# The first mixer of a two-layer kernel: short attention products to GpSimd, low parts of weights to VectorE, casts and two score levels to ScalarE, linear attention's outputs in four parts

## The chip, the cores and the metric

The kernel runs on one core of one Trainium2 chip. The metric is the device time of one execution in microseconds (us). The core has five engines that run their own queues in order and wait for each other by semaphores: TensorE (PE in the profile; its weight loads are PEld), VectorE (DVE), ScalarE (ACT), GpSimd (POOL) and SyncE (SP), which here issues nearly all DMA transfers.

## The reference, cut to what matters

The reference computes two transformer layers on 256 tokens of width 1024 (and 16 meta tokens ahead of them, so 272 rows). The first layer begins with a hybrid mixer, and only this mixer is touched by the change:

```python
proj = hn @ w_in                      # 1024 x 3088: sbq sbk sbv | gq gk gv gr glr
sb_o = stick_breaking_attention(...)  # 8 heads of 64
#   a = exp(log_sigmoid(z) + sum over later keys of log_sigmoid(-z)), strictly causal
lg = log_sigmoid(glr @ w_gate_up + b_gate_up) / 16
gla_o = gated_linear_attention(...)   # 4 heads, key width 64, value width 128
#   attn[t,s] = sum_d q[t,d] k[s,d] exp(bcum[t,d] - bcum[s,d]), causal;  o = attn @ v
gla_o = rmsnorm(gla_o, gla_norm_g) * silu(gr)
h = h + concat([rmsnorm(sb_o), gla_o]) @ w_out
```

After it come an expert layer (product keys, 16384 single-neuron experts, all of them multiplied through) and a second layer with window attention, a linear recurrence and a feed-forward part. All data is float32.

## The kernel before

**Weights as jobs.** Every weight matrix passes through as a stream of jobs of 128x1024 elements. A job is loaded by DMA into a buffer `raw` (four of them), split into a high part `whi` (a rounding cast to the type fp32r, line 194) and a low part `wlo = raw - whi` (a subtraction, line 196), and multiplied in three passes (lines 48 to 50: high by high, high by low, low by high). `whi` and `wlo` have three buffers each. A letter per job says who splits it: a lower-case letter puts the cast on ScalarE, an upper-case one on VectorE; `p` or `P` puts the subtraction on GpSimd, `v` or `V` on VectorE. In the first mixer the letters are the string in `lo_cycle(...)` of `plan_mixer1`, one per job; the mixer has 33 jobs: 4 for sbq, 4 for sbk, 4 for sbv, a small one for glr, 2 for gk, 2 for gq, 4 for gv, 4 for gr and 8 for `w_out` (called k=0 to k=7).

**Steps.** `st.step(mid)` runs one job. It first emits the copies that evacuate finished results, then loads up to the sixth job ahead and splits up to the second job ahead, and then emits the job's matmuls in two halves; between the halves it calls `mid`. So what stands in `mid`, and what stands behind the step, is woven between the matmul halves of TensorE's queue. The weaving is done with Python generators; `run(g)` emits one piece of g up to its next `yield`. The order of all queues is therefore fixed by the order of these calls.

**Attention** (`sb_units`, nine steps, jobs 8 to 16). There are 12 units, each one or two heads of one block of 128 queries. In each half step a unit passes a stage: scores on TensorE (line 458); sigmoid on ScalarE (431) and the causal mask on GpSimd (433, an affine select); one minus it, a running product over the keys on VectorE (440, 442) and the product with the shifted result (443); transposes on TensorE (450) and a small copy; and copies out of PSUM (422, 424, 425).

**Linear attention** (`gla`, eight steps, jobs 17 to 24). The 128x128 decay matrix of a block is built in levels: level v treats blocks of 2h columns, h = 2^v, and multiplies keys of the first half of each block with queries of the second half. A level has four stages in four successive half steps: differences `Dt` on VectorE (622) and two exponentials on ScalarE (623, 624); products `kq` with keys and queries (631, 632); 8 matmuls on TensorE into two PSUM banks (644); and two masked copies (`copy_predicated`, line 616) that put the level's entries into `AT`. The two PSUM banks of a level have only these two buffers, so the next level's matmuls wait for the copies. Between these pieces stands the output part of the first attention, `sb_out` (so), which multiplies weights with values (541, 546), and normalises (555 to 575), and `v_rows` (vr), which transposes gv (483).

**Outputs of linear attention** (`gla_out`). For each block of 128 rows and each of four heads it multiplies `Amt`, `AT` and for the second block `Axt` with values (694, 695, 697); then the rows are normalised in `head_norm` (470 to 475, the power on GpSimd at line 83), transposed (104) and split (112, 113) into `mixT`. The `w_out` job k=4 is the first that needs them; k=5 to 7 are held and multiplied at the end. Behind the mixer stand the residual addition (1078), the next norm, and the first jobs of the expert layer.

Of the kernel before, what the change touches and what calls it, by code (L numbers as in the profile page):

```python
# [14 lines left out]
ALU = mybir.AluOpType  # L15
# [149 lines left out]
class Job:  # L165
# [33 lines left out]
    def mm(self):  # L199
        self.f(self.W)  # L200
# [170 lines left out]
def lo_cycle(pat):  # L371
    while True:
        yield from pat
# [31 lines left out]
def sb_units(cx, sm, sbqT, sbkT, A0T, A1T, bm):  # L405
# [4 lines left out]
    nc = cx.nc  # L410
# [3 lines left out]
    for u in range(nu + 4):  # L414
# [11 lines left out]
        if 0 <= u - 1 < nu:  # L426
            i, hd = units[u - 1]
            n = 144 + 128 * i
# [6 lines left out]
        if 0 <= u - 2 < nu:  # L435
            i, hd = units[u - 2]
            n = 144 + 128 * i
            be = bs[u - 2]
            sc = sm.tile([128, 288], F32, tag="sc", name="sc", bufs=2)[:, :n * len(hd)].rearrange("p (h k) -> p h k", h=len(hd))
            nc.vector.tensor_scalar(out=sc, in0=be, scalar1=-1.0, scalar2=1.0, op0=ALU.mult, op1=ALU.add)  # L440
            for j in range(len(hd)):
                nc.vector.tensor_tensor_scan(sc[:, j, ::-1], sc[:, j, ::-1], cx.zero[:, :n], 1.0, ALU.mult, ALU.add)  # L442
            nc.vector.tensor_tensor(out=be[:, :, 0:n - 1], in0=be[:, :, 0:n - 1], in1=sc[:, :, 1:n], op=ALU.mult)
        if 0 <= u - 3 < nu:
            i, hd = units[u - 3]
            be = bs.pop(u - 3)
# [134 lines left out]
def gla(cx, sm, P, mk):  # L581
# [3 lines left out]
    nc = cx.nc  # L585
# [22 lines left out]
    def blocks(a, h):  # L608
        return a.rearrange("p a (n c) -> p (a n) c", c=2 * h)

    for lv in range(8 + 3):

        v = lv - 3
        if v >= 0:
            for b in range(2):
                nc.vector.copy_predicated(P.AT[:, b], mk[:, v, :].unsqueeze(1).broadcast_to((128, 4, 128)),
                                          pas.pop((v, b)).rearrange("p (a t) -> p a t", a=4))
        if lv < 7:
            h = 1 << lv
            Dt = sm.tile([128, 2, 256], F32, tag="Dt", name="Dt", bufs=2)  # L620
# [6 lines left out]
        if 0 <= v < 7:  # L627
            h = 1 << v
            kq = sm.tile([128, 2, 256], F32, tag="kq", name="kq", bufs=2)
            d, o = blocks(Ds.pop(v), h), blocks(kq, h)  # L630
            nc.vector.tensor_tensor(out=o[:, :, 0:h], in0=d[:, :, 0:h], in1=blocks(P.kR, h)[:, :, 0:h], op=ALU.mult)
            nc.vector.tensor_tensor(out=o[:, :, h:], in0=d[:, :, h:], in1=blocks(P.qR, h)[:, :, h:], op=ALU.mult)
            KQ[v] = kq, kq
        elif v == 7:
            KQ[v] = P.kR, P.qR
# [19 lines left out]
            nc.vector.tensor_tensor(out=km, in0=P.bm, in1=P.bm[:, :, 15:16].broadcast_to((128, 2, 16)), op=ALU.subtract)  # L655
            nc.scalar.activation(km, km, AF.Exp, scale=-S)
        if lv == 9:
            nc.vector.tensor_tensor(out=P.QE, in0=P.QE, in1=P.qR, op=ALU.mult)
            nc.vector.tensor_tensor(out=P.KE0, in0=P.KE0, in1=P.kR[:, :, 0:128], op=ALU.mult)
            km = P.KEm[:, :, 0, :]  # L660
            nc.vector.tensor_tensor(out=km, in0=km, in1=P.km, op=ALU.mult)
            nc.vector.tensor_tensor(out=P.KEm[:, :, 1, :], in0=km, in1=P.e0.unsqueeze(2).broadcast_to((128, 2, 16)), op=ALU.mult)
# [21 lines left out]
def gla_out(cx, sm, P, mixT):  # L684
    nc = cx.nc
    mm = nc.tensor.matmul
    pos = []
    for i in range(2):
        po = cx.bank("t")
        for h in range(4):  # L690
            vs = slice(128 * h, 128 * h + 128)
            o = po[:, vs]
            b, j = h % 2, h // 2
            mm(o, P.Amt[:, b, 2 * i + j, :], P.gvm[:, vs], start=(h == 0), stop=False, skip_group_check=True)
            mm(o, P.AT[:, b, 2 * i + j, :], P.gv[:, i, vs], start=False, stop=(h == 3 and i == 0), skip_group_check=True)
            if i == 1:
                mm(o, P.Axt[:, 2 * b + j, :], P.gv[:, 0, vs], start=False, stop=(h == 3), skip_group_check=True)
        pos.append(po)
    yield
    rw = [sm.tile([128, 512], F32, tag="rw", name="rw", bufs=4) for _ in range(2)]  # L700
    ns = [head_norm(cx, sm, pos[i], 4, 128, P.sg[:, i, :], rw[i]) for i in range(2)]
    for _ in range(2):
        for n in ns:
            run(n)
        yield
    for i in range(2):
        cx.dump(f"rowgl{i}", rw[i])
    pv = [cx.tr_pe(rw[i], 128) for i in range(2)]
    yield
    for i in range(2):  # L710
        cx.tr_split(pv[i], mixT, 4, 128 * i)


def plan_mixer1(cx, st, M):
    I = cx.I
    W = I["w_in"][0]
    nc = cx.nc
    lo = lo_cycle("pvpVpvpvPVVPVppVPPpvpPppPpPvppVVv")
    xT = lambda: M.hT
    tiles = lambda: [tuple(a[:, :, 16 + 128 * i:144 + 128 * i] for a in M.hT) for i in range(2)]  # L720

# [10 lines left out]
    def ev_g(i, ps):  # L732
        g, t = M.P.sg[:, i, :], cx.sm.tile([128, 512], F32, tag="rw", name="rw", bufs=4)
        nc.scalar.activation(g, ps, AF.Sigmoid)
        nc.vector.tensor_tensor(out=t, in0=ps, in1=M.ggl, op=ALU.mult)  # L735
        st.defer(lambda: nc.gpsimd.tensor_tensor(out=g, in0=g, in1=t, op=ALU.mult))


    def glr(W_):
# [20 lines left out]
def mixer1(cx, st, M, hx):  # L760

    nc, tc, I = cx.nc, cx.tc, cx.I
    if True:
# [93 lines left out]
        vr = v_rows(cx, M.vT, P.gv, P.gvm, "z")  # L857
        lc = lru_consts(cx)
        for n in range(8):
            st.step(adv(g, so) if n < 7 else adv(g))  # L860
            run(so if n < 6 else vr)
            run(g)
            run(lc)
        go = gla_out(cx, sm, P, M.mixT)
        st.step(adv(g))
        run(vr)
        run(g)
        for n in range(7):
            st.step(adv(go))
            run(go)  # L870
            if n == 3:
                g2 = peer_gain(cx)
        drain(go)
        peer_in(cx, st, M, hx, g2)
# [1000 lines left out]
```

## Time and profile before

| | us |
|---|---|
| Time before, median of 3 runs (lowest, highest) | 1306.52 (1304.94, 1306.63) |
| The profiled execution: its device time | 1307.48 |
| Its span, first to last instruction | 1305.8 |
| TensorE matmuls busy | 1246.6 (95%) |
| VectorE busy | 978.8 (75%) |
| ScalarE busy | 682.0 (52%) |
| GpSimd busy | 590.8 (45%) |

The device time holds 1.7 us that lie outside the span. All stretches below are in microseconds from the start of the span: the stick-breaking attention lies from about 36 to 84, the linear attention from 84 to 145, the `w_out` jobs with the linear attention's outputs from 145 to 181, and the expert layer begins at about 188.

### The profile page before, as it was taken

To read this page: it belongs to the slowest core of one execution; us is meant where nothing else is said; L and a number is where in the kernel's file an instruction comes from. 1 tells how busy PE (TensorE), PEld (TensorE's weight loads), DVE (VectorE), ACT (ScalarE), POOL (GpSimd) and SP (SyncE) were. 2 spreads that over 40 slices of the span, in tenths; PEclk is the share of its full clock that TensorE was granted. 3 is DMA by queue.
4 is the path that set the end of the run, shared out by engine and by line. 5 is a ranking of instruction groups with operands and counts; after the bars stand their busy time and mean duration, and the time that the engine had idled before them with its cause. 6 is when DMAs were issued, how large, how long until landed. Compare 5 with 4: busy or idle time off the path is not lost.

```text
span 1305.8 us, 23107 instructions
## 1 busy us (share of the span) xinstructions
PE 1246.6 (95%) x8724; PEld 1103.2 (84%) x8724; DVE 978.8 (75%) x1556; ACT 682.0 (52%) x1381; POOL 590.8 (45%) x291
## 2 busy tenths in 40 slices
PE   8988889989999999999999999999997989999998
PEld 7876679989999999998777788888886977999886
DVE  5778366998999888887899986555557887676444
ACT  5343244444456777776776774445544633545222
POOL 4433334778888777776666566000003342200101
PEclk9999799999999999999999999999998989899999
DMA  7431158656666656663554546765554423456653
GB/s 224 129 97 65 65 146 206 177 162 178 188 175 187 178 171 171 171 178 113 178 179 144 166 167 205 228 230 183 188 192 114 134 81 97 146 179 192 191 187 105
DMA packets 147292, 211.10 MB, mean 162 GB/s; under 512 B 17559, under 2 KB 121165, under 8 KB 147182
## 3 DMA queue, kind: packets, MB, share of 16 engines
q1 hardware_dynamic: 146844, 209.41, 53.3%
q8 instruction: 68, 1.11, 0.4%
q14 instruction: 42, 0.34, 0.1%
q10 hardware_dynamic: 338, 0.23, 0.1%
HBM read 207.35 MB, written 2.10 MB: 160 GB/s over the span
## 4 chain that ended last, share of the span: by engine, by line
PE 73%; DVE 11%; issue 7%; POOL 5%; ACT 2%; DMA 2%; SPq 0%; DVEq 0%; POOLq 0%; ACTq 0%
PE mm L48 22%; PE mm L49 22%; PE mm L50 22%; POOL wlo L196 3%; PE pg L1041 2%; POOL wlo L224 1%; DVE sc L442 1%; DVE whi L194 1%; DVE wlo L196 1%; PE z L1513 1%; DMA raw<-in_w_peer_q_dram 1%; DVE ut L215 1%; DMA g<-in_norm_g_dram 1%; PE t L644 1%; PE t L1531 1%
## 5 line engine op out<-in xcount | busy, mean ns | idle before, releaser
L196 POOL TENSOR_TENSOR wlo<-raw,whi 128x1024 fp32r<-128x1024 f32 x98 | 241.4, 2470 | 352.4 <-ACT whi L194 276.1
L224 POOL TENSOR_TENSOR wlo<-ut,whi 128x1024 fp32r<-128x1024 f32 x128 | 307.0, 2407 | 84.4 <-ACT whi L223 81.7
L194 ACT CAST whi<-raw 128x1024 fp32r<-128x1024 f32 x208 | 217.3, 1049 | 194.5 <-PE mm L50 154.4
L196 DVE TENSOR_TENSOR wlo<-raw,whi 128x1024 fp32r<-128x1024 f32 (+1 forms) x157 | 198.5, 1267 | 150.7 <-ACT whi L194 147.8
L50 PE MATMUL mm<-xTh,wlo 128*128 128x256 f32 x1088 | 305.1, 280 | 3.3 <-POOL wlo L224 3.3
L48 PE MATMUL mm<-xTh,whi 128*128 128x256 f32 x1088 | 306.5, 282 | 1.6 <-ACT whi L223 1.4
L49 PE MATMUL mm<-xTl,whi 128*128 128x256 f32 x1088 | 304.4, 280 | 0.3 <-DVE xTl L113 0.3
L49 PE MATMUL mm<-wlo,xTh 128*128 128x512 f32 x576 | 230.1, 400 | 4.2 <-POOL wlo L196 4.1
L48 PE MATMUL mm<-whi,xTh 128*128 128x512 f32 x576 | 232.1, 403 | 0.3 <-DVE rw L735 0.3
L50 PE MATMUL mm<-whi,xTl 128*128 128x512 f32 x576 | 229.1, 398 | 0.0
L50 PEld LDWEIGHTS mm<-xTh,wlo 128*128 128x128 f32 x1088 | 205.0, 188 | 3.9 <-POOL wlo L224 3.9
L48 PEld LDWEIGHTS mm<-xTh,whi 128*128 128x128 f32 x1088 | 204.6, 188 | 2.4 <-ACT whi L223 1.6
L49 PEld LDWEIGHTS mm<-xTl,whi 128*128 128x128 f32 x1088 | 205.0, 188 | 0.5 <-DVE xTl L113 0.5
L215 DVE STREAM_TRANSPOSE ut<-raw 128x1024 f32<-128x1024 f32 x128 | 158.7, 1240 | 39.2 <-POOL wlo L224 24.6
L223 ACT CAST whi<-ut 128x1024 fp32r<-128x1024 f32 x128 | 133.7, 1045 | 52.0 <-DVE ut L215 26.2
L1047 ACT ACTIVATE A<-A,w 128x64 f16<-128x64 f16 x512 | 129.1, 336 | 32.5 <-DVE A L1025 32.4
L49 PEld LDWEIGHTS mm<-wlo,xTh 128*128 128x128 f32 x576 | 109.4, 190 | 31.9 <-POOL wlo L196 7.2
L48 PEld LDWEIGHTS mm<-whi,xTh 128*128 128x128 f32 x576 | 109.4, 190 | 26.9 <-DVE rw L735 0.8
L50 PEld LDWEIGHTS mm<-whi,xTl 128*128 128x128 f32 x576 | 109.3, 190 | 26.6 <-DVE xTl L1210 0.4
L1210 DVE TENSOR_TENSOR xTl<-HS,xTh 128x256 fp32r<-128x256 f32 (+1 forms) x129 | 98.7, 767 | 3.3 <-ACT xTh L1206 3.3
L1114 ACT ACTIVATE HS<-mm 128x512 f32<-128x512 f32 x64 | 38.4, 599 | 86.5 <-PE mm L50 86.4
L1045 DVE TENSOR_TENSOR B<-kc,i 128x1024 f16<-128x1024 f32 x64 | 76.9, 1201 | 5.2 <-PE pg L1041 5.2
(394 smaller groups left out, 2059.5 us busy)
## 6 DMA issues: line engine op xcount, KB each, us to landing
raw<-in_expert_u_dram SPq DMA_DIRECT2D x512, 128.0 KB, 3.0
raw<-in_expert_v_dram SPq DMA_DIRECT2D x128, 512.0 KB, 3.5
raw<-in_w_ff_dram SPq DMA_DIRECT2D x64, 512.0 KB, 3.9
raw<-in_w_in_dram SPq DMA_DIRECT2D x38, 512.0 KB, 3.9
raw<-in_w_out_dram SPq DMA_DIRECT2D x16, 512.0 KB, 3.4
raw<-in_w_peer_q_dram SPq DMA_DIRECT2D x32, 128.0 KB, 4.4
h1d<-row SPq DMA_DIRECT2D x2, 512.0 KB
row<-h1d SPq DMA_DIRECT2D x2, 512.0 KB, 5.8
```

The lines of the kernel that those rows point to most:

```text
L48: mm(out, lhs[0], rhs[0], start=start, stop=False, skip_group_check=sk)
L49: mm(out, lhs[0], rhs[1], start=False, stop=False, skip_group_check=sk)
L50: mm(out, lhs[1], rhs[0], start=False, stop=stop, skip_group_check=sk)
L194: (nc.vector.tensor_copy if self.lo.isupper() else nc.scalar.copy)(hi[:, :n], self.raw[:, :n])
L196: eng.tensor_tensor(out=lo[:, :n], in0=self.raw[:, :n], in1=f32(hi[:, :n]), op=ALU.subtract)
L215: self.cx.nc.vector.transpose(self.ut, self.raw)
L223: nc.scalar.copy(ov(hi), pv(ut))
L224: nc.gpsimd.tensor_tensor(out=ov(lo), in0=pv(ut), in1=ov(f32(hi)), op=ALU.subtract)
L1045: nc.vector.tensor_tensor(out=B, in0=G.iota.unsqueeze(1).broadcast_to((128, 8, 128)), in1=bc(G.i2[:, c], 128), op=ALU.is_equal)
L1047: nc.scalar.activation(A[0][:, j, :], A[0][:, j, :], AF.Copy, scale=G.w1[:, t0 + j:t0 + j + 1])
L1114: st.defer(lambda: nc.scalar.activation(M.HS[b // NH][:, o - 1:o + 1, :].rearrange("p a t -> p (a t)"), ph, AF.Gelu))
L1210: nc.vector.tensor_tensor(out=wl[:, ts], in0=src(b, ts), in1=f32(wh[:, ts]), op=ALU.subtract)
```

## The change

Six edits, all in the first mixer:

- In `sb_units` the product of line 443 goes from VectorE to GpSimd (12 instructions of 271 or 286 elements per partition).
- In `gla` the two products `kq` of each of seven levels go from VectorE to GpSimd (14 instructions of 256 elements), and two later products, `QE` (512) and `KE0` (256).
- The masked copies of levels 5 and 6 become plain copies of the blocks that matter, on ScalarE: four of 32 partitions for level 5, two of 64 for level 6.
- The string of the weight splits changes from job 8 on: all casts on ScalarE; all subtractions on VectorE but for jobs 26, 28 and 29.
- The product of `sg` with its gain (line 736 before) goes from GpSimd to VectorE.
- `gla_out` yields after every second head, so its matmuls stand in four parts and not in one, and it begins one step earlier; `sb_out` and `v_rows` are woven in another order.

```diff
-            nc.vector.tensor_tensor(out=be[:, :, 0:n - 1], in0=be[:, :, 0:n - 1], in1=sc[:, :, 1:n], op=ALU.mult)
+            nc.gpsimd.tensor_tensor(out=be[:, :, 0:n - 1], in0=be[:, :, 0:n - 1], in1=sc[:, :, 1:n], op=ALU.mult)
...
-                nc.vector.copy_predicated(P.AT[:, b], mk[:, v, :].unsqueeze(1).broadcast_to((128, 4, 128)),
-                                          pas.pop((v, b)).rearrange("p (a t) -> p a t", a=4))
+                pa = pas.pop((v, b)).rearrange("p (a t) -> p a t", a=4)
+                if v in (5, 6):
+
+                    h = 1 << v
+                    for s in range(0, 128, 2 * h):
+                        nc.scalar.copy(P.AT[s:s + h, b, :, s + h:s + 2 * h], pa[s:s + h, :, s + h:s + 2 * h])
+                else:
+                    nc.vector.copy_predicated(P.AT[:, b], mk[:, v, :].unsqueeze(1).broadcast_to((128, 4, 128)), pa)
...
-            nc.vector.tensor_tensor(out=o[:, :, 0:h], in0=d[:, :, 0:h], in1=blocks(P.kR, h)[:, :, 0:h], op=ALU.mult)
-            nc.vector.tensor_tensor(out=o[:, :, h:], in0=d[:, :, h:], in1=blocks(P.qR, h)[:, :, h:], op=ALU.mult)
+            nc.gpsimd.tensor_tensor(out=o[:, :, 0:h], in0=d[:, :, 0:h], in1=blocks(P.kR, h)[:, :, 0:h], op=ALU.mult)
+            nc.gpsimd.tensor_tensor(out=o[:, :, h:], in0=d[:, :, h:], in1=blocks(P.qR, h)[:, :, h:], op=ALU.mult)
...
-            nc.vector.tensor_tensor(out=P.QE, in0=P.QE, in1=P.qR, op=ALU.mult)
-            nc.vector.tensor_tensor(out=P.KE0, in0=P.KE0, in1=P.kR[:, :, 0:128], op=ALU.mult)
+            nc.gpsimd.tensor_tensor(out=P.QE, in0=P.QE, in1=P.qR, op=ALU.mult)
+            nc.gpsimd.tensor_tensor(out=P.KE0, in0=P.KE0, in1=P.kR[:, :, 0:128], op=ALU.mult)
...
+            if h % 2:
+                yield
         pos.append(po)
-    yield
...
-    lo = lo_cycle("pvpVpvpvPVVPVppVPPpvpPppPpPvppVVv")
+    lo = lo_cycle("pvpVpvpv" + 17 * "v" + "vpvppvvv")
...
-        st.defer(lambda: nc.gpsimd.tensor_tensor(out=g, in0=g, in1=t, op=ALU.mult))
+        st.defer(lambda: nc.vector.tensor_tensor(out=g, in0=g, in1=t, op=ALU.mult))
...
-            st.step(adv(g, so) if n < 7 else adv(g))
-            run(so if n < 6 else vr)
+            st.step(adv(g, vr if n == 6 else so))
+            run(vr if n in (4, 5) else so)
             run(g)
             run(lc)
+        run(so)
+        drain(g)
         go = gla_out(cx, sm, P, M.mixT)
-        st.step(adv(g))
-        run(vr)
-        run(g)
-        for n in range(7):
+        for n in range(8):
             st.step(adv(go))
             run(go)
-            if n == 3:
+            if n == 4:
                 g2 = peer_gain(cx)
```

GpSimd's queue over the attention, before (`be` is a unit's weights, `wlo` a job's low part):

```order
L196 TENSOR_TENSOR wlo<-raw,whi 128x1024
L433 AFFINE_SELECT be<-be 128x128 x2
L196 TENSOR_TENSOR wlo<-raw,whi 128x1024
L433 AFFINE_SELECT be<-be 128x128 x3
L196 TENSOR_TENSOR wlo<-raw,whi 128x1024
L433 AFFINE_SELECT be<-be 128x128 x2
```

The same place in the changed kernel:

```order
L433 AFFINE_SELECT be<-be 128x128
L443 TENSOR_TENSOR be<-be,sc 128x271
L433 AFFINE_SELECT be<-be 128x128
L443 TENSOR_TENSOR be<-be,sc 128x271
L433 AFFINE_SELECT be<-be 128x128
L443 TENSOR_TENSOR be<-be,sc 128x271
```

The long subtractions are gone from this stretch, and a product of one unit now stands behind the mask of the next unit.

VectorE's queue in the step that takes the differences of levels 4 and 5, before:

```order
L622 TENSOR_TENSOR Dt<-bR 128x512
L631 TENSOR_TENSOR kq<-Dt,kR 128x32x8
L632 TENSOR_TENSOR kq<-Dt,qR 128x32x8
L616 COPY_PREDICATED AT<-mk,t 128x512 x2
L622 TENSOR_TENSOR Dt<-bR 128x512
L631 TENSOR_TENSOR kq<-Dt,kR 128x16x16
L632 TENSOR_TENSOR kq<-Dt,qR 128x16x16
```

The same place in the changed kernel (line 623 is the masked copy, 628 the difference, 1274 a constant of the second layer):

```order
L196 TENSOR_TENSOR wlo<-raw,whi 128x1024
L623 COPY_PREDICATED AT<-mk,t 128x512 x2
L628 TENSOR_TENSOR Dt<-bR 128x512
L623 COPY_PREDICATED AT<-mk,t 128x512 x2
L628 TENSOR_TENSOR Dt<-bR 128x512
L1274 SCALAR_TENSOR_TENSOR sp<-sp,z_1060 128x4 x2
L196 TENSOR_TENSOR wlo<-raw,whi 128x1024
```

The two products between two masked copies have left VectorE; once in two levels a subtraction of the weights stands ahead of a masked copy.

TensorE's queue at the outputs of linear attention, before (part of 20 short matmuls that stand in one run):

```order
L694 MATMUL t<-gvm,Amt 128x128
L695 MATMUL t<-gv,AT 128x128
L697 MATMUL t<-gv,Axt 128x128
L694 MATMUL t<-gvm,Amt 128x128
L695 MATMUL t<-gv,AT 128x128
L697 MATMUL t<-gv,Axt 128x128
L694 MATMUL t<-gvm,Amt 128x128
L695 MATMUL t<-gv,AT 128x128
```

In the changed kernel (lines 700, 701, 703 are the old 694, 695, 697):

```order
L50 MATMUL mm<-whi,xTl 128x512
L700 MATMUL t<-gvm,Amt 128x128
L701 MATMUL t<-gv,AT 128x128
L703 MATMUL t<-gv,Axt 128x128
L700 MATMUL t<-gvm,Amt 128x128
L701 MATMUL t<-gv,AT 128x128
L703 MATMUL t<-gv,Axt 128x128
L48 MATMUL mm<-whi,xTh 128x512
```

Two heads stand between two halves of a `w_out` job where all eight stood in a row. SyncE issues the same transfers in the same order before and after.

## Rows read from the trace of the kernel before

**Rows 1.** The page: span, and busy time of each engine.

```profile
span 1305.8 us, 23107 instructions
PE 1246.6 (95%) x8724; PEld 1103.2 (84%) x8724; DVE 978.8 (75%) x1556; ACT 682.0 (52%) x1381; POOL 590.8 (45%) x291
```

**Rows 2.** Busy time by stretch: start:end, length, then PE, PEld, DVE, ACT, POOL, clock, DMA.

```profile
84.00:145.10 61.10, 52.49 (x361) 39.65 (x361) 45.25 (x80) 21.31 (x48) 17.57 (x7) 0.92 0.25 78
145.10:181.30 36.20, 35.86 (x147) 27.55 (x144) 17.43 (x23) 9.97 (x16) 10.66 (x6) 0.86 0.38 102
```

**Rows 3.** What TensorE waited for, 0 to 200: total, times, longest.

```profile
PE t L644 <- DVE AT L616: 4.3, 3, 3.8
PE t L104 <- DVE xr L129: 3.3, 1, 3.3
PE z L483 <- DVE xTl L113: 3.2, 1, 3.2
PE z L450 <- DVE be L443: 2.4, 1, 2.4
...
PE t L644 <- DVE kq L632: 0.9, 1, 0.9
```

**Rows 4.** TensorE in three stretches of low clock: length, PE busy, clock.

```profile
118.83:122.24 3.41, 3.29 (x18) 0.53 0.01 2
135.89:142.72 6.83, 6.02 (x28) 0.51 0.26 79
152.96:163.20 10.24, 10.24 (x33) 0.51 0.15 51
```

**Rows 5.** TensorE's timeline: two pairs of output matmuls, start, duration.

```profile
151.33 0.49 PE L695 MATMUL t<-gv,AT 128*128 128x128 f32 x2
...
156.20 0.80 PE L695 MATMUL t<-gv,AT 128*128 128x128 f32 x2
```

**Rows 6.** Timeline of all engines, 96.5 to 100.

```profile
96.98 2.71 POOL L196 TENSOR_TENSOR wlo<-raw,whi 128x1024 fp32r<-128x1024 f32 x1 [4.09 <-PE t L644]
...
97.37 2.61 DVE L631 TENSOR_TENSOR kq<-Dt,kR 128x256 f32<-128x256 f32 x1
```

**Rows 7.** Groups of VectorE's instructions, 36 to 182: count | busy, mean ns.

```profile
L616 DVE COPY_PREDICATED AT<-mk,t 128x512 f32<-128x512 int32 x16 | 10.7, 720 | 0.3 <-PE t L644 0.2
L196 DVE TENSOR_TENSOR wlo<-raw,whi 128x1024 fp32r<-128x1024 f32 x8 | 10.3, 1288 | 6.6 <-ACT whi L194 6.1
...
L631 DVE TENSOR_TENSOR kq<-Dt,kR 128x256 f32<-128x256 f32 x7 | 7.3, 1040 | 0.0
...
L632 DVE TENSOR_TENSOR kq<-Dt,qR 128x256 f32<-128x256 f32 x7 | 2.9, 412 | 0.0
...
L424 DVE COPY A0T<-z 128x128 f32<-128x128 f32 x8 | 2.3, 284 | 0.4 <-PE z L450 0.4
```

**Rows 8.** Groups of GpSimd's instructions over the whole span.

```profile
L196 POOL TENSOR_TENSOR wlo<-raw,whi 128x1024 fp32r<-128x1024 f32 x98 | 241.4, 2470 | 352.4 <-ACT whi L194 276.1 <-DVE whi L194 43.3 <-issue 16.5
...
L433 POOL TENSOR_SCALAR_AFFINE_SELECT be<-be 128x128 f32<-128x128 f32 x8 | 3.4, 423 | 7.6 <-ACT be L431 7.6
...
L1405 POOL TENSOR_TENSOR sq<-sq,tr 128x544 f32<-128x544 f32 x1 | 1.3, 1332 | 2.8 <-DVE tr L1404 2.8
```

**Rows 9.** Groups of ScalarE's instructions, 36 to 182.

```profile
L194 ACT CAST whi<-raw 128x1024 fp32r<-128x1024 f32 x12 | 12.6, 1046 | 9.7 <-issue 5.0 <-PE mm L50 3.1 <-PE mm L49 1.0
L431 ACT ACTIVATE be<-z 128x272 f32<-128x272 f32 x8 | 3.2, 403 | 0.8 <-PE z L458 0.7
...
L425 ACT COPY A1T<-z 128x128 f32<-128x128 f32 x8 | 2.1, 267 | 13.3 <-DVE A0T L424 13.3
```

**Rows 10.** The chain that ended last, pieces between 76 and 137.

```profile
76.63 2.41 DVE be L443
...
112.34 2.52 DVE kq L631
...
117.76 1.25 DVE AT L616 x2
...
129.38 2.52 DVE KE L659
```

**Rows 11.** TensorE's timeline: the attention scores of two units, one step apart.

```profile
52.80 0.72 PE L458 MATMUL z<-sbkT,sbqT 64*128 64x272 f32 x2
...
57.94 0.72 PE L458 MATMUL z<-sbkT,sbqT 64*128 64x272 f32 x2
```

## The prediction

> **What bounds the kernel now.** I read the page first: TensorE's matmuls are busy 1246.6 of 1305.8 us [rows 1], so what can be won is TensorE's idle time and the time in which its clock is low. The change touches only the first mixer, so I then read the busy times by stretch. In the linear attention TensorE works 52.49 of 61.10 us, and its mean clock is 0.92; in the outputs stretch it is hardly idle (35.86 of 36.20), but its clock is 0.86 [rows 2]. The list of TensorE's waits says what the idle time is: it waits 4.3 us for the masked copies into `AT`, 3.2 for a low part at the end of the stick-breaking outputs, 2.4 for the last product of the attention and 0.9 for `kq`; all four releasers are VectorE [rows 3]. The chain of work shows why VectorE is late: ahead of the masked copies and of that low part it holds a product of 2.52 us each, and the attention's last product took 2.41 [rows 10], where an undisturbed product of the same size as `kq` takes 0.41 [rows 7]. The timeline gives the reason: the long product began at 97.37, while GpSimd was in a subtraction of the weights from 96.98 to 99.69, and ended 0.3 us after it [rows 6]. So GpSimd's 2.4 us subtractions block VectorE's instructions that read two operands from SBUF, and each one delays whatever chain TensorE waits for. The last view is the clock: three stretches of 3.41, 6.83 and 10.24 us run at about 0.5 [rows 4], which is 1.2 of 2.4 GHz. The first two begin right after the two long waits; the third begins in the run of short output matmuls, where TensorE does not wait.
>
> **The sum: what goes.** (a) *Waits in linear attention, 4.3 + 3.2 + 0.9 = 8.4 us* [rows 3]. VectorE loses per step of two levels the four products of 2 x (1.04 + 0.41) = 2.9 us and takes one subtraction of 1.29 us in their place [rows 7], so its own work falls by 1.6 us a step; and no 2.47 us subtraction [rows 8] stands on GpSimd there, so the blocked 2.5 us pieces cannot come back at that length. On TensorE's side the next level's matmuls wait only for two masked copies of 2 x 0.72 [rows 7]; that fits into the half step between two levels, which is half of the 5.14 us that I read for a step of the attention [rows 11], an estimate for this stretch. Levels 5 and 6 leave VectorE altogether. I take the whole 8.4.
>
> (b) *The last product of the attention, 2.4 us* [rows 3]. It goes to GpSimd. No row shows GpSimd on 271 elements. The nearest is a product of 544 elements at 1.33 us [rows 8], half of it 0.67; if a part of that is a fixed cost, as much as 0.85. I take 0.75. Blocked it took 2.41 [rows 10], so 1.65 us of the wait go.
>
> (c) *The low clock.* TensorE is busy 3.29 + 6.02 + 10.24 = 19.55 us in the three stretches [rows 4]. At the full clock that work takes between half (if only the clock counts) and 0.49/0.80 = 0.61 of it (as a pair of output matmuls measures at either level [rows 5]); so 7.6 to 9.8 us are lost, and I take 8.6. The first 9.31 us of these come with the waits of (a) and should go with them. For the third stretch the reason is open; the change puts weight matmuls between the parts.
>
> Together 8.4 + 1.65 + 8.6 = 18.65 us.
>
> **What is paid back.** (d) *Attention steps.* The product now stands in GpSimd's queue behind the mask of the next unit, that behind a sigmoid, that behind a copy on ScalarE which waits for VectorE's copy of the same bank, and that stands on VectorE behind the job's subtraction, which waits for ScalarE's cast. From the end of a job's matmuls: cast 1.05, subtraction 1.29, copies 0.28 and 0.27, sigmoid 0.40, mask 0.42, product 0.75 [rows 7 to 9], 4.46 us, against 5.14 us until the transposes of that unit are due, one step later [rows 11]. An evacuation of results ahead of the cast, which comes in about every second job, adds some 0.4 to 0.7. So it just fits; semaphores and a collision with VectorE may cost 0 to 0.3 us in each of nine steps. I take 1.0. (e) *Linear attention.* VectorE's subtraction now heads its queue in every step, the masked copies behind it, and TensorE waits for those. Cast, subtraction and two masked copies are 1.05 + 1.29 + 1.44 = 3.8 us, against the second half's pieces, and the next half job; about 0 to 0.5 us in each of two or three steps. 1.0. GpSimd's products of one level (2 x 0.65, estimated from the same 544-element row) have a half step to themselves. (f) *Norms of the outputs.* They have twelve `w_out` matmuls and half a job as cover; GpSimd's power stands behind the subtraction of job 29, 2.47 us [rows 8]. 0.5. (g) *Clock.* I let one short low stretch stay somewhere, 1.5 us (of 3.41, half).
>
> The remaining edits I cost at nothing: ScalarE's added casts of 1.05 us (about a dozen) and block copies lie in an engine that is busy 21.31 of 61.10 us there [rows 2]; without that cover each would be worth 1 us. The product of `sg` on VectorE is due only after the first output parts. SyncE's order of transfers is unchanged, and the 3.3 us that TensorE waits behind the mixer for `xr` [rows 3] stay, since they are a chain of the last results.
>
> Paid back 1.0 + 1.0 + 0.5 + 1.5 = 4.0, net gain 14.65. The profiled execution took 1307.48 us (span 1305.8), so 1292.8; it lies 1.0 above the median of the runs, so I expect **1291.8**.
>
> **Rivals.** *1. The low clock stays in the output parts.* For it: the third stretch began without a wait [rows 3, 4], and the same short matmuls, part of the 33 instructions there, still have to run. Against it: they stand between weight matmuls now. It would leave 10.24 x 0.42 = 4.3 us, and 1.5 of that I already paid: 1294.6. *2. New lock waits.* Short products on GpSimd now meet VectorE's subtractions and running products of every unit. If each product waits out one subtraction of 1.29 us [rows 7], the chain of (d) is 5.75 us against 5.14, 0.6 us a step and 5.5 in nine; the same in six steps of linear attention, 3.6, would also hold some of the low clock, 2: 1291.8 + 11.1 - 2.0 already paid, 1301. The Trainium skill names this in SBUF — State Buffer, "SBUF: two separate sides": the pair of ports that both share is locked for a whole instruction by whichever comes first. The blocked product agrees with it [rows 6]. *3. The slow engine.* GpSimd takes 1.33 us for 544 elements, 2.45 ns each [rows 8], VectorE 0.41 for 256, 1.61 ns [rows 7]. The 28 moved products have about 7650 elements, so they become 0.84 ns x 7650 = 6.4 us longer in all; if TensorE waited for all of it, the time would be 1298.2. Against it: what hurt was a long instruction on GpSimd, and the short ones come in its place, in other half steps than the matmuls that need them. The Trainium skill has this as a rule that speaks against the change: GPSIMD Engine Reference, section "Performance versus the Vector engine", calls GpSimd the wrong engine for ordinary elementwise arithmetic, VectorE being roughly twice as fast. The trace agrees on the long subtraction, 2.47 us against 1.29 [rows 7, 8]. *4. Slower than before.* One mechanism: the attention's loop over four engines (d) does not fit by far. To eat the whole gain, nine steps must each become 14.65/9 = 1.6 us longer, that is, the chain must take 5.14 + 1.6 = 6.8 where I add up 4.5; from 7.0 on the kernel is over 0.2% slower. That needs two collisions of a subtraction's length in every step; 1310 to 1312. *5. Nothing changes*, because the weight stream or the end chain holds the mixer's end: against it, TensorE has no wait for a transfer of weights in the list [rows 3]. 1306.
>
> **How the numbers follow.** Forecast (gain 10.5 to 19, 1287.5 to 1296) 0.50, and rival 1, which lies in the same span, 0.12. Everything hidden, the full 18.65 or a little more, 1285 to 1288: 0.09. Rival 2 or a part of it (1296 to 1303) 0.13, rival 3 0.05. No change (within 0.2%, 2.6 us, about what a measurement of this kernel can tell from none), rival 5 and the worst of rival 2, 0.05. Slower, rival 4, 0.06. So 0.89 faster. The range for 8 in 10 reaches over the hidden case and into rival 2, up to 1300: 1286.5 to 1300. The likeliest case's own range is 1287.5 to 1296.
>
> **What would show it.** In the profile after: TensorE's waits for `AT`, for the low part and for the last attention product are each under 1 us; no VectorE product of 2.5 us in 40 to 145; the clock is 1.0 from 36 to the mixer's end, and one output pair takes 0.49 everywhere; the first job of the expert layer starts about 15 us earlier. Wrong would be: waits of TensorE for `be` (transposes) in most attention steps, which is (d) and rival 2 or 3; waits for `AT` behind a subtraction, which is (e); or a clock at half in the outputs, which is rival 1.

## The result and the profile after

The kernel after takes 1291.85 us (median of 4 runs, 1290.42 to 1292.9) against 1306.58 (4 runs, 1304.94 to 1308.89): 0.9888 of the time, 95% interval 0.9871 to 0.9906. It is faster by 14.7 us; 1291.8 was forecast. The profiled execution took 1292.9 us, its span is 1290.9.

All of it lies in the mixer. In the following rows of the view by stretch (columns as in [rows 2]) each stretch runs from the first attention scores to the end of the last `w_out` matmul of line 48, which in every kernel ends 0.5 us before the mixer's last matmul; first the kernel before, then the kernel after:

```profile
40.16:180.84 140.68, 128.91 (x786) 101.80 (x786) 97.74 (x162) 48.05 (x113) 48.30 (x31) 0.93 0.31 91
```

```profile
40.84:165.84 125.00, 120.28 (x786) 95.03 (x786) 80.07 (x137) 61.11 (x133) 37.81 (x45) 0.99 0.35 103
```

I call this length *the stretch* below, since it is compared for every kernel. It fell by 15.7 us: TensorE's idle time from 140.68 - 128.91 = 11.8 to 4.7 us, and the busy time of its same 786 matmuls from 128.9 to 120.3, mostly by the clock (0.93 to 0.99). It begins 0.7 us later than before. What follows the stretch took 1125.0 us before and 1125.1 after.

By stage, against [rows 2], linear attention and the outputs:

```profile
83.85:134.20 50.35, 48.06 (x359) 36.75 (x359) 34.66 (x63) 26.10 (x58) 16.01 (x17) 0.97 0.28 87
134.20:166.30 32.10, 31.40 (x145) 23.54 (x143) 17.90 (x25) 13.08 (x20) 7.22 (x5) 1.00 0.42 116
```

The outputs, hardly idle before either, run at the full clock now. The list of TensorE's waits from 0 to 200 answers to [rows 3]:

```profile
PE t L104 <- DVE xr L129: 2.3, 1, 2.3
PE t L650 <- POOL kq L638: 2.0, 1, 2.0
PE z L450 <- POOL be L443: 1.4, 1, 1.4
PE t L104 <- ACT xTh L112: 0.7, 1, 0.7
...
PE t L650 <- DVE AT L623: 0.3, 1, 0.3
```

The wait for `AT` is down to 0.3 and the one for `xTl` is gone. But `kq` got longer (0.9 to 2.0) and the last attention product still costs 1.4. Of the three stretches of [rows 4] none is left; one new one stands at 97.3, right behind the wait for `kq`:

```profile
97.30:100.70 3.40, 3.40 (x16) 2.00 (x14) 3.40 (x5) 1.19 (x4) 1.20 (x3) 0.50 0.23 47
```

The groups of GpSimd's instructions from 36 to 166, against [rows 8]:

```profile
L443 POOL TENSOR_TENSOR be<-be,sc 128x271 f32<-128x271 f32 (+1 forms) x12 | 8.8, 730 | 8.0 <-DVE sc L442 7.3 <-DVE sc L440 0.4
...
L637 POOL TENSOR_TENSOR kq<-Dt,kR 128x256 f32<-128x256 f32 x7 | 6.1, 874 | 26.6 <-ACT Dt L629 18.1 <-PE t L650 5.9 <-ACT Dt L630 2.7
L638 POOL TENSOR_TENSOR kq<-Dt,qR 128x256 f32<-128x256 f32 x7 | 5.8, 833 | 0.0
```

The products take what was estimated for `be` (0.73 against 0.75) and more for `kq` (0.85 against 0.65). Why TensorE waits for the first `kq` is read from the chain of work that ended last (start, length, what):

```profile
87.99 0.66 ACT ge L600
...
88.88 1.04 ACT whi L194
...
89.95 1.23 DVE wlo L196
91.17 0.65 DVE gt L602
...
93.32 0.70 DVE Dt L628
...
94.04 0.45 ACT Dt L629
...
94.56 0.84 POOL kq L637
95.40 0.81 POOL kq L638
...
96.25 0.82 PE t L650 x9
```

A job's subtraction (89.95) waits for its cast, the cast stands behind the gate's exponentials on ScalarE, and the gate's own work on VectorE (`gt`, the scans, `Dt`) is queued behind the subtraction. The wait for `be` at 78.7 reads the same way on the timelines of VectorE and, last line, GpSimd: its input is late because a subtraction at 75.49 stands ahead, and the product itself is then 0.66:

```profile
75.49 1.23 DVE L196 TENSOR_TENSOR wlo<-raw,whi 128x1024 fp32r<-128x1024 f32 x1 [1.84 <-ACT whi L194]
...
77.16 0.72 DVE L442 TENSOR_TENSOR_SCAN sc<-sc,zero 128x272 f32<-128x272 f32 x1
...
78.03 0.66 POOL L443 TENSOR_TENSOR be<-be,sc 128x271 f32<-128x271 f32 x1 [3.84 <-DVE sc L442]
```

### The profile page after: what moved, and what is told of

It reads as the page before. It is cut to its first block, busy times and chain, and to the rows that moved or that the text cites. A ratio compares the mean times of both kernels' runs of the same rounds, so it can differ in the third digit from the quotient of the medians.

```text
span 1290.9 us, 23130 instructions
## 1 busy us (share of the span) xinstructions
PE 1239.4 (96%) x8724; PEld 1097.8 (85%) x8724; DVE 956.5 (74%) x1526; ACT 696.2 (54%) x1400; POOL 577.2 (45%) x304
## 4 chain that ended last, share of the span: by engine, by line
PE 79%; DVE 9%; issue 5%; POOL 3%; ACT 2%; DMA 1%; SPq 1%; DVEq 0%; POOLq 0%; ACTq 0%
PE mm L48 24%; PE mm L49 24%; PE mm L50 24%; PE pg L1047 2%; POOL wlo L196 1%; POOL wlo L224 1%; DVE wlo L196 1%; DVE xTl L1216 1%; PE z L1519 1%; PE t L650 1%; ACT whi L194 1%; PE z L458 1%; DVE ut L215 1%; DVE B L1051 1%; PE t L1537 1%
## 5 line engine op out<-in xcount | busy, mean ns | idle before, releaser
L196 POOL TENSOR_TENSOR wlo<-raw,whi 128x1024 fp32r<-128x1024 f32 x85 | 208.5, 2461 | 316.4 <-ACT whi L194 257.3
L196 DVE TENSOR_TENSOR wlo<-raw,whi 128x1024 fp32r<-128x1024 f32 x170 | 214.0, 1261 | 177.6 <-ACT whi L194 175.0
L194 ACT CAST whi<-raw 128x1024 fp32r<-128x1024 f32 x221 | 230.2, 1045 | 204.5 <-PE mm L50 166.1
```

Source lines behind the costliest of these rows:

```text
L194: (nc.vector.tensor_copy if self.lo.isupper() else nc.scalar.copy)(hi[:, :n], self.raw[:, :n])
L196: eng.tensor_tensor(out=lo[:, :n], in0=self.raw[:, :n], in1=f32(hi[:, :n]), op=ALU.subtract)
```

## The experiments

The theory carried into them is the prediction's: the long waits came from GpSimd's subtractions, which block VectorE's products, so letters and products make the gain. The rivals: the new order of `sb_out`, `v_rows` and the outputs makes it; or the four parts do; or the two levels on ScalarE. Each kernel undoes one part or does one alone. A trace is one execution, while a time is the median of several, and the two differ by some us between executions; so each verdict gives both. How much a total can move without the change is seen behind the stretch: the same code took 1120.6 us there in the trace of e9 and 1126.0 in that of e10.

**e1, the old string** in the kernel after:

```diff
-    lo = lo_cycle("pvpVpvpv" + 17 * "v" + "vpvppvvv")
+    lo = lo_cycle("pvpVpvpvPVVPVppVPPpvpPppPpPvppVVv")
```

> The changed kernel with the old string of weight splits: long subtractions return to GpSimd, casts to VectorE; products stay on GpSimd, outputs in four parts. Lock theory (long GpSimd subtractions block VectorE's two-operand work, and now also stand ahead of GpSimd's own products): TensorE's waits in linear attention come back to 6 us or more, at least one low-clock stretch with them, the mixer's last matmul ends at 174 to 180 us and not 166, 1299 to 1306 us. Load theory (VectorE merely had too much to do): VectorE has even less work than in the changed kernel, so 1290 to 1293. Weave theory (the new order and the four parts give the gain): 1291 to 1294.

Measured: 1296.67 us, ratio 0.9928 (0.9899 to 0.9957); stretch 128.4. TensorE waits 2.5 for `be`, 2.3 for `kq`, 2.1 for `gv`; `AT` is not among its waits. That lies between the ranges of the three theories. Against the kernel after the new letters are worth 4.8 us by the medians, and two thirds of the gain stays without them.

**e2, the new string alone**, in the kernel before (the same two lines the other way round).

> The kernel before with only the new string of weight splits: no long subtraction on GpSimd in the attention, all products still on VectorE, outputs in one run. Lock theory: no VectorE product of 2.5 us any more, but VectorE now has all the work, so half of the waits go: 1298 to 1303 us, and the low-clock stretch in the outputs stays. Load theory: more work on VectorE, so slower than before, 1308 or more. Weave theory: 1306, no change.

Measured: 1303.83 us, ratio 0.9983 (0.9968 to 0.9998); stretch 132.9 in its trace, which is that of its fastest run. TensorE still waits for `AT`, now 3.0 in sum, and 1.7 for `xTl`. Without long subtractions on GpSimd in these steps, 4.7 of the 7.5 us of waits ascribed to them remain. The 3.0 are two waits: 1.7 where it was 3.8, and a new one of 1.3 at 105, where a job's subtraction on VectorE (103.18 to 104.41) now stands ahead of the masked copies.

**e3, the order alone**, with the four parts, in the kernel before; products, letters and levels are old:

```diff
-            st.step(adv(g, so) if n < 7 else adv(g))
-            run(so if n < 6 else vr)
+            st.step(adv(g, vr if n == 6 else so))
+            run(vr if n in (4, 5) else so)
...
+            if h % 2:
+                yield
```

> The kernel before with only the new weave and the outputs in four parts. Lock theory: the waits of TensorE for VectorE stay at 6 us or more; the low clock in the outputs goes, worth 4 to 5 us: 1301 to 1303. Weave theory: 1292 to 1297. If the clock in the outputs stays low all the same: 1306.

Measured: 1295.06 us, ratio 0.993 (0.9904 to 0.9957); stretch 130.4. That is 9 us of the gain by the ratio and 11.6 by the medians, with the blocked products `be` and `kq` as long as before (means of 1224 and 1042 ns, line 631). Only the third, `KE` (2.60 us at 129.30 in the kernel before), takes 0.41 here: it starts at 127.63, after GpSimd's subtraction has ended (124.81 to 127.16). The two next fences show why, on VectorE's timeline around one level; first the kernel before, then e3:

```profile
112.25 2.62 DVE L631 TENSOR_TENSOR kq<-Dt,kR 128x256 f32<-128x256 f32 x1
114.79 0.41 DVE L632 TENSOR_TENSOR kq<-Dt,qR 128x256 f32<-128x256 f32 x1
115.12 0.41 DVE L559 TENSOR_SCALAR sbx<-z 8x256 f32<-8x256 f32 x1
116.46 0.41 DVE L563 TENSOR_TENSOR sbt<-sbx,sbr 8x256 f32<-8x256 f32 x1 [0.93 <-ACT sbr L561]
116.91 0.41 DVE L564 SCALAR_TENSOR_TENSOR sbt<-sbt,sbr 8x256 f32<-8x256 f32 x1
117.35 0.41 DVE L565 SCALAR_TENSOR_TENSOR sbr<-sbt,sbr 8x256 f32<-8x256 f32 x1
117.69 1.31 DVE L616 COPY_PREDICATED AT<-mk,t 128x512 f32<-128x512 int32 x2
```

```profile
113.45 2.62 DVE L631 TENSOR_TENSOR kq<-Dt,kR 128x256 f32<-128x256 f32 x1
115.99 0.41 DVE L632 TENSOR_TENSOR kq<-Dt,qR 128x256 f32<-128x256 f32 x1
116.33 0.41 DVE L559 TENSOR_SCALAR sbx<-z 8x256 f32<-8x256 f32 x1
116.66 1.33 DVE L616 COPY_PREDICATED AT<-mk,t 128x512 f32<-128x512 int32 x2
```

The blocked product is 2.62 us in both, 2.2 more than the 0.41 of the one behind it. In the kernel before the first attention's normalisation (`sbt`, `sbr`), with a wait for two ScalarE functions, stands between it and the masked copy that TensorE waits for: from the end of `sbx` to the copy 117.69 - 115.53 = 2.2 us. In e3 it comes at 122.3, the copy follows `sbx` at once, and TensorE has no wait for `AT` here. That takes 2.2 of the 3.8 us; where the rest went is seen on TensorE, again before and then e3:

```profile
114.27 0.39 PE L50 MATMUL mm<-whi,hTl 128*128 128x512 f32 x1
118.45 2.68 PE L644 MATMUL t<-kq 64*128 64x128 f32 x16 [3.80 <-DVE AT L616]
```

```profile
115.46 0.39 PE L50 MATMUL mm<-whi,hTl 128*128 128x512 f32 x1
115.69 0.60 PE L483 MATMUL z<-ident,vT 128*128 128x128 f32 x4
116.79 0.66 PE L483 MATMUL z<-ident,vT 128*128 128x128 f32 x4 [0.50 <-DVE sbx L559]
117.43 1.77 PE L644 MATMUL t<-kq 64*128 64x128 f32 x16
```

The new order puts the eight transposes of the value rows into this place. They fill 1.2 us of it, and a wait of 0.5 for `sbx` stands between them.

**e4, the outputs in one run** in the kernel after (the two `yield` lines of e3 the other way).

> The changed kernel with the outputs of linear attention in one run again (20 short matmuls in a row), begun one step early as in the change. If the run of short matmuls itself lowers the clock: a stretch of half clock in it, plus 3 to 5 us, 1295 to 1297. If the clock there was low only in the wake of the earlier waits: full clock, 1291 to 1293.

Measured: 1295.46 us, ratio 0.9929 (0.9901 to 0.9957); stretch 128.2. The low clock is back among the output matmuls, without a wait before it, and the norms, with less cover, cost 1.6 us of wait instead of 0.7:

```profile
140.30:147.10 6.80, 6.80 (x23) 5.35 (x22) 1.19 (x5) 0.60 (x1) 1.05 (x2) 0.50 0.16 65
```

So the parts are worth 3.6 us by the medians. But a run alone does not decide the clock: the traces of e2 and e9 have the outputs in one run too, and there it stays at 1.00. Both are traces of the execution with the highest mean clock of their kernel (0.982, where the ten of e2 have 0.973 to 0.982, and 0.985, where the twelve of e9 have 0.974 to 0.985), so other executions may have it low there. Of four traces with one run two show the low clock inside it; of ten with four parts none does.

**e5, all 28 products back on VectorE** in the kernel after (`nc.vector` for `nc.gpsimd` at lines 443, 637, 638, 664, 665).

> The changed kernel with all 28 products back on VectorE; the new string of splits, the levels on ScalarE and the four parts stay. Lock theory: nothing long on GpSimd, so no blocked products, but VectorE's queue is longer by about 2 us a step: the waits for the masked copies return in part, 1293 to 1297 us. Load theory: most of the gain is gone, 1300 or more. Weave theory: 1291 to 1293.

Measured: 1290.64 us, ratio 0.9857 (0.984 to 0.9873); stretch 124.0. Not slower than the kernel after. TensorE's waits: `AT` 1.3, `be` 1.2, `kq` 1.1. The two groups of `kq` take 0.41 us each here:

```profile
L443 DVE TENSOR_TENSOR be<-be,sc 128x271 f32<-128x271 f32 (+1 forms) x12 | 5.4, 447 | 0.6
...
L638 DVE TENSOR_TENSOR kq<-Dt,qR 128x256 f32<-128x256 f32 x7 | 2.9, 415 | 0.0
L637 DVE TENSOR_TENSOR kq<-Dt,kR 128x256 f32<-128x256 f32 x7 | 2.9, 414 | 0.0
```

**e6, levels 5 and 6 back on VectorE** in the kernel after (`if v in ():` for `if v in (5, 6):`).

> The changed kernel with levels 5 and 6 as masked copies on VectorE again. I costed this edit at nothing beyond the waits: VectorE is given 4 x 0.73 us in two half steps, ScalarE loses 1.7. If VectorE has room there: 1291 to 1293, TensorE's waits for the copies under 0.5 us. If these levels were the tight place: waits of 1 to 3 us for them, 1293 to 1296.

Measured: 1292.93 us, ratio 0.9879 (0.9862 to 0.9895), which cannot be told from the kernel after. Its trace, of a run of 1296.62, has a stretch of 128.1 with `AT` waits of 0.9 in sum, more than the 0.5 expected, and one more low-clock stretch, at 131.3; the other three runs are at 1292.8 to 1293.0. So the levels are worth about 1 us, if anything.

**e7 and e8, later subtractions**, a test of the reading of the two waits that are left. In e7 job 20 is split behind the first level's `Dt`, in the middle of its step; e8 does that with job 17 too, in the attention's eighth step.

```diff
-    def step(self, mid=None):
+    def step(self, mid=None, ahead=3):
         self.flush()
-        self.fill(6, 3)
+        self.fill(6, ahead)
...
+            if n == 1:
+                st.step(lambda: (run(g), st.fill(5, 2), run(so)), 2)
+            else:
+                st.step(adv(g, vr if n == 6 else so))
```

> The changed kernel, in which one job's split (cast and subtraction of job 20) is emitted behind the first level's differences and not ahead of the gates' scans. My reading of the trace after: VectorE's queue holds this subtraction, which waits for ScalarE's cast, ahead of the gates, so that kq comes 2 us late; and the low-clock stretch at 97 begins with that wait. If so, the wait for kq falls from 2.0 to under 0.4 us, the stretch at 97 goes (1.5 us), and the time falls by 3 to 4 us, 1288 to 1289. If GpSimd's two products of 0.84 us or the exponentials set the place: 1 us or less.

> The same, and also the split of job 17 emitted behind the last attention unit's running product. The last product then starts 1.2 us or more earlier: TensorE's wait for it falls from 1.4 to under 0.3 us, so 1.2 to 1.5 us less than the kernel with one split moved, 1286.5 to 1288. If the wait is the sigmoid's or the mask's instead: no difference between the two.

Measured: e7 1292.91 us, ratio 0.9876 (0.986 to 0.9893), stretch 125.1; e8 1291.72 us, 0.9867 (0.985 to 0.9883), stretch 123.7. In e7 the wait for `kq` and the low clock at 97 are gone, in e8 that for `be` too: the reading of both was right. The times expected (1288 to 1289, 1286.5 to 1288) were missed: the time is the same, since waits for `AT` came in their place, 2.7 and 3.0 us in sum. VectorE's timeline of e8 shows how: a subtraction, which waits for its cast, now heads the masked copies.

```profile
102.06 1.56 DVE L196 TENSOR_TENSOR wlo<-raw,whi 128x1024 fp32r<-128x1024 f32 x1 [0.19 <-ACT whi L194]
103.55 1.31 DVE L623 COPY_PREDICATED AT<-mk,t 128x512 f32<-128x512 int32 x2
```

**e9, the order without the four parts**, in the kernel before (e3 without the two `yield` lines).

> The kernel before with only the new order of the steps around linear attention; its outputs stay in one run, its split string, products and levels are the old ones. Theory that the order alone removes the long waits (the masked copy no longer stands behind the first attention's normalisation, and the transposes of the value rows come a step earlier): TensorE's waits for AT are 0.5 to 1.2 us in sum and the 3.2 us wait for xTl is gone, although products of 2.5 us still stand on VectorE; a low-clock stretch of 6.8 us lies in the outputs, as in the kernel with one run; the stretch from the first attention scores to the last output matmul is 133 to 135 us (140.7 before, 130.4 with the four parts), the time 1297 to 1300 us. Rival, the four parts carry the gain: AT stays at 3.5 to 4.5 us, the stretch is 137 or more, 1302 us or more. Rival, the blocked products carry it: AT stays at 3.5 or more, as in the kernel with new letters alone.

Measured: 1300.49 us (12 runs, 1293.68 to 1305.65), ratio 0.995 (0.9932 to 0.9967); stretch 133.1. `AT` and `xTl` as expected: 0.6 and 0; the transposes of the value rows wait 0.5 for `sbx` and 0.6 for `gv` instead. The low clock that was expected in the outputs did not come in this trace; TensorE waits 3.7 us for the norms (`rw`). The order alone gives 6.5 us by the ratio and 7.0 by the medians, the parts 2.6 and 5.4 on top.

**e10 and e11, all subtractions later**: e8, with the same edit for the steps n = 1 to 5; e11 with the products on VectorE.

```diff
-            if n == 1:
+            if 1 <= n <= 5:
```

> The kernel after, with the splits of job 17 and of the jobs of five steps of linear attention emitted behind the vector pieces of the same step (two jobs ahead instead of three, in the middle of the job). Theory that each of TensorE's waits for AT is a masked copy that stands in VectorE's queue behind a subtraction and its cast: waits for AT fall from 3.0 us (with two splits later) to 0.5 or less, be and kq stay at 0, no low-clock stretch before the outputs, and the stretch is 120.5 to 122.5 us (125.0 after); the time is 1287 to 1290 us. Rival, the late splits come too late for their own job: TensorE waits 0.5 us or more for wlo, or in three or more steps for the cast, and the time is 1291.5 us or more.

> The same with all 28 attention products on VectorE instead of GpSimd. Theory that a product costs 0.41 to 0.5 us on VectorE once no long subtraction of GpSimd blocks it, against 0.73 to 0.84 on GpSimd, and that both fit: within 0.15% of the run before this one, and of the two this one not the slower by more than 0.1%. Rival, VectorE is full: waits for AT or be of over 1 us come back, and it is 1 us or more slower than with the products on GpSimd.

Measured: e10 1293.91 us, ratio 0.9899 (0.9875 to 0.9923), stretch 126.5; e11 1292.47 us, 0.989 (0.9869 to 0.9912), stretch 126.5. The theory of e10 fell and the rival's time came, though not by the waits that it named: TensorE does not wait for `wlo`, the late splits cost elsewhere. One wait for `AT` of 2.0 stays, and two new ones come for copies of the value rows, `gv` 2.3 and `sbx` 1.1. VectorE's timeline before the longest of them:

```profile
120.33 1.66 DVE L196 TENSOR_TENSOR wlo<-raw,whi 128x1024 fp32r<-128x1024 f32 x1 [3.58 <-ACT whi L194]
121.91 0.41 DVE L563 TENSOR_TENSOR sbt<-sbx,sbr 8x256 f32<-8x256 f32 x1
...
123.14 1.27 DVE L489 COPY gv<-z 128x512 f32<-128x512 f32 x2
```

VectorE sits idle for 3.58 us ahead of a subtraction whose cast on ScalarE ends at 120.3, and the rest of the normalisation and the copies that TensorE waits for are queued behind it. e11 is the faster of the two by 1.4 us, as its expectation allows.

**e12, products on VectorE and the old string**: the kernel after without its two first edits, so with the order, the four parts, the levels and the product of `sg`.

> The kernel after with the products on VectorE and the old string of splits: subtractions of 2.47 us on GpSimd again stand beside products on VectorE, with the new order, the four parts and two levels on ScalarE. Theory by overlap: the blocked products come back (be at 2.4, kq at 0.9 us), AT stays under 1 us since the order keeps it short, the stretch is 127 to 129 us and the time 1293.5 to 1296, so that the old string costs 3 to 4 us here as it does with the products on GpSimd (128.4 us, 1296.7). Rival of the prediction, the block of the port is the main cause: the old string costs 6 us or more here, and waits for AT of 2 us or more return.

Measured: 1294.6 us, ratio 0.9904 (0.988 to 0.9927); stretch 125.9. Its row by stretch, its groups of products on VectorE, and its waits:

```profile
39.70:165.70 126.00, 120.40 (x786) 94.83 (x786) 97.82 (x161) 49.93 (x120) 45.16 (x29) 1.00 0.34 102
```

```profile
L443 DVE TENSOR_TENSOR be<-be,sc 128x271 f32<-128x271 f32 (+1 forms) x12 | 11.6, 969 | 0.6
...
L637 DVE TENSOR_TENSOR kq<-Dt,kR 128x256 f32<-128x256 f32 x7 | 7.3, 1037 | 0.0
```

```profile
PE z L450 <- DVE be L443: 2.4, 1, 2.4
PE t L650 <- DVE kq L638: 0.8, 1, 0.8
...
PE z L483 <- DVE gv L489: 0.6, 1, 0.6
PE z L483 <- DVE sbx L559: 0.5, 1, 0.5
```

With e3 and e9 this run decides. VectorE is as busy as in the kernel before (97.8 against 97.7 us), its first `kq` product as long (1037 ns against 1040 in [rows 7]), the string of the subtractions is the old one; and yet TensorE does 140.7 us of the mixer in 126.0, less than the 127 to 129 expected. The waits for `AT` and `xTl`, 7.5 us before, are gone; the blocked `be` of 2.4 us is still there. Of the blocked products only `KE` is short here too, 0.41 us.

## Why the number was right and a reason was not

**(a) The waits in linear attention: the size came out near, half of the reason failed.** They fell by 8.4 - 2.3 = 6.1 us of the 8.4 taken. The step that failed is the one that ascribes them to VectorE's load and to GpSimd's subtractions alone, "so the blocked 2.5 us pieces cannot come back at that length". In e3, e9 and e12 the blocked `kq` is there and VectorE's load is the old one, and the waits for `AT` (4.3) and `xTl` (3.2) are nearly or wholly gone; in e2 the pieces are gone, and 3.0 and 1.7 us of waits remain. Shown is that the order removes them (e9 changes nothing but the order, with the outputs' earlier begin). For `AT` the fences at e3 show how: the block and the normalisation behind it delayed the copy by 2.2 us each. With the block taken out (e2) 1.7 of the 3.8 is left at this level. With the normalisation taken out (e3) 1.6 would be left, and there the transposes of the value rows fill it, but for 0.5 of wait. For `xTl` it is the same move: these transposes needed a PSUM bank that the first attention's output held until that low part, and in e3 they run at 115.7 to 117.4, some 10 us ahead of `KE` (127.63) and of that output. So the short `KE` of e3, e9 and e12 has no part in it, while in e2, where the transposes are late, the short `KE` leaves 1.7 of 3.2. The block was a real part of both waits, 2.1 and 1.5 us by e2; with the new order TensorE hardly waits behind it any more at these places (e12). The prediction read the piece of the chain with the largest number [rows 10] as the cause and did not ask what else lay between it and the wait; and it costed the order of `sb_out` and `v_rows` at nothing, without a sentence.

The 0.9 us for `kq` became 2.0: a product on GpSimd takes 0.85 and two of them stand in line, and ahead of them stands the subtraction now on VectorE (chain above; e7 removes the wait by moving that one split).

**(b) The last product of the attention: too large.** 1.65 us were to go, 1.0 did. The product takes 0.66, less than the 0.75 taken; what was missed here is that its input comes later, behind the subtraction that changed engines (e8: with that split moved, no wait).

**(c) and (g) The low clock: 1.5 us more than forecast.** TensorE's busy time in the stretch fell by 128.9 - 120.3 = 8.6 us, against 8.6 lost in three stretches less 1.5 let stay, 7.1. One short stretch did stay, at 97.3. The two stretches at the long waits went with the waits (in e9 too); the second had begun before its wait ended and not behind it (0.81 of its 6.83 us are idle [rows 4]). The third went with the four parts as far as e4 shows; since e2 and e9 have no low clock in their one run, what lowers it there stays open. It also differs between executions of one kernel: the kernel before, beside e1 to e4, ran in 1301.68 us at a mean clock of 0.979 and in 1314.03 at 0.971. So a size read from one pair of traces holds for that pair.

**(d) Attention steps: 1.0 paid back in nine steps, measured in one.** The only such wait left is the last, the 1.4 of (b), and it is the chain of (d), a subtraction ahead on VectorE; the wait for `A1T` is 0.3 where it was 0.4. The 0 to 0.3 us a step for semaphores and collisions was a guess that no row gives. **(e) Masked copies behind a subtraction: 1.0, measured 0.3** in the kernel after, but with the mechanism right: e7 and e8 make it 2.7 and 3.0, and the 2.0 for `kq` comes from a subtraction ahead as well. **(f) Norms: 0.5, measured 0.7.**

So in the traces idle time fell by 7.1 us where the terms (a), (b), (d), (e), (f) make 7.55, and busy time by 8.6 where (c) and (g) make 7.1. That the forecast is met within 0.1 us is luck: the parts miss by up to 1.5 us in both directions, and runs of one kernel lie 2.5 us (after) and 4 us (before) apart. Of the signs that the prediction asked for, two failed: the wait for the last product is 1.4 and not under 1, and the clock is 0.50 at 97.3.

**What each edit is worth**, in a ladder of medians (ratios at each run): before 1306 to 1308; order 1300.5; with the four parts 1295.1; with levels and `sg` 1294.6; with the letters too 1290.6; with the products on GpSimd 1291.85. The steps are 7.0, 5.4, 0.5, 4.0 and -1.2 us by these medians and 6.5, 2.6, 3.4, 6.1 and -4.0 by the ratios; the kernels ran beside different runs of the kernel before, and the two accounts agree on the signs and on the order's part, not on the smaller sizes. The steps do not add in another order: the letters give 2.8 us alone and 4.0 to 4.8 behind the rest, and e7 and e8 show why this can be: where one wait goes, another comes. The product of `sg` and the earlier begin of the outputs were not tested alone. What the change's first words name, the products on GpSimd, gives nothing beside the new order: in three pairs that differ in it alone (e5 and after, e12 and e1, e11 and e10) VectorE is the better place by 1.2, 2.1 and 1.4 us by the medians. Each pair's intervals overlap; that all three have one sign is the only evidence that it is better and not equal. No run has the products alone in the kernel before, where they would have met the blocks.

**Rivals.** 1 did not come (the outputs run at 1.00). 2, 4 and 5 did not. 3, the slow engine, is there with the sign that was given and a fifth to a third of its price of 6.4: `kq` takes 874 and 833 ns on GpSimd against 414 and 415 on VectorE. The Trainium skill (GPSIMD Engine Reference, "Performance versus the Vector engine") calls VectorE roughly twice as fast for elementwise work; the 874 against 414 agree, and the three pairs lean the same way.

**What stays open.** No version is shown to beat the kernel after beyond doubt: e5 is 0.3% lower by its ratio, with overlapping intervals. The remaining waits, about 4 us in the stretch, moved in e7, e8 and e10 with the subtraction to whatever it then stood ahead of.

## What to carry to other kernels

A long blocked instruction on the chain is not yet the cause of a wait: list everything that stands between it and the instruction waited for, and test the cheapest edit, the order, alone. In an engine that runs in order, an instruction that waits for another engine's result costs the idle time ahead of it to all that is queued behind; in e7, e8 and e10 moving it moved the wait. When several edits land together, undo each from the full version and also try each alone: here the one named first was worth nothing beside the others.

## What the runs showed of the hardware

The block between the two engines works both ways. A subtraction on VectorE that began at 96.97 took 1.90 us beside GpSimd's `kq` products, one at 89.95 with GpSimd idle 1.23:

```profile
96.95 0.85 POOL L638 TENSOR_TENSOR kq<-Dt,qR 128x256 f32<-128x256 f32 x1
96.97 1.90 DVE L196 TENSOR_TENSOR wlo<-raw,whi 128x1024 fp32r<-128x1024 f32 x1 [0.76 <-ACT whi L194]
```

So short products on GpSimd hurt VectorE less than long subtractions did, 0.7 us here and not 2.2, but they are not free. And the same run of output matmuls ran at a granted clock of 0.50 for 6.8 us in e4 and at 1.00 throughout in e2 and e9. Nor does a wait of TensorE settle what follows: behind the wait for `be` of 2.4 to 2.5 us the clock fell to 0.50 for 3.4 us in e1, e3 and e9 (at 80.4, 79.0 and 81.0) and stayed at 1.00 in the kernel before and in e12; behind the wait for `kq` of 2.0 it fell in the kernel after and in e6 and not in e4.
